# A trunk kernel on one core: P of two head groups turned by VectorE and DRAM instead of TensorE, a hand-ordered opening, and moved waits

## The chip, the cores and the metric

The kernel runs on one core of a Trainium2 chip. The core has five engines that run their own instruction queues in order: PE (TensorE, matmuls and transposes), DVE (VectorE), ACT (ScalarE), POOL (GpSimd) and SP (SyncE, which here only issues DMAs); ACT issues DMAs too. The metric is the device time of one execution in microseconds (us).

## The reference

Two layers over `x` (256 rows, width 1024), all in float32. Each layer is a half-step SwiGLU, a mixer, and another half-step SwiGLU. The mixer of layer 0 is the one that the change touches most:

```python
x = x + 0.5 * swiglu(rmsnorm(x, ffn1_norm[i]), w_gate, w_up, w_down)   # D_FF = 2816
h = rmsnorm(x, mix_norm[i])
q_s, k_s, v_s, q_m = split(h @ w_in[i])            # widths 768, 768, 768, 256
k_m, v_m = split(rmsnorm(mem, mem_norm[i]) @ w_mem_kv[i])
q_m, k_m = rmsnorm per head of 64                  # 4 memory heads, 256 keys
o_m = softmax(q_m k_m^T / 8) v_m
# layer 0: 12 heads of 64, chunks of 64 rows, each sees its own and earlier chunks
q, k = rmsnorm(q_s), rmsnorm(k_s)
s = q k^T / 8 + rel_bias[head, clip(row - key, -128, 128) + 128]
o_s = softmax(where(key chunk <= row chunk, s, -1e30)) v
# layer 1: differential attention with rotary q and k, 6 heads of 2 x 64
x = x + concat(o_s, o_m) @ w_out[i]
x = x + 0.5 * swiglu(rmsnorm(x, ffn2_norm[i]), ...)
```

## The kernel before

Every large product is made of three passes of 128x512 on PE: with a weight split into `hi` (its fp32r cast) and `lo` (the rest), and the activations likewise into `xh` and `xl`, the passes are hi·xh (L542), lo·xh (L545) and hi·xl (L548). Weights arrive by SP's DMAs in three `raw` buffers (L321), ACT casts `hi` (L367), DVE subtracts `lo` (L385). Some products of the feed-forward parts are made by Strassen sums, which the change leaves alone.

The order of the instructions on every engine is fixed when the program is built. A planner, `Flow`, runs generators ("threads"): each emits instructions, adds their cost to a planned clock (`flow.pe`, `flow.act`, `flow.dve`), and yields either a planned time at which it wants to go on or a condition (a free buffer, a free PSUM bank). Between two products of the main stream the planner lets those threads emit whose time or condition has come. So a thread's `yield flow.now + 5.0` decides only where its next instructions stand in the queues; on the chip an instruction waits for what it reads, and holds what is behind it on its engine.

**First mixer.** `qk_evac` (L1380 on) takes a projection's PSUM bank, makes squares on ACT (`sq`), sums and a power on DVE and POOL, and the normalized `qkn` on DVE (L1049); PE transposes it into `qktp` (L578), ACT and DVE copy it with its gain. q's rows are transposed by `flip`, a reversed identity, which turns their order around: so the bias of row p and key j can be read from a table by a plain stride (`load_bias`), and the P of a head group is turned back by the same `flip`. `attn_soft` makes the scores of four heads (`S`, L1487), adds the bias and takes maxima on DVE, exponentials on ACT (L1538), scales on DVE, then `p_transpose` turns P on PE into the bank `ptp` with 128x128 transposes against `flip`, ACT copies it to `PT` (L1501), and `AV` follows (L1571), with a cast on ACT and a subtract on DVE into `oT`. There are three head groups (12 heads), each for two row tiles of 128; tile 0 sees 128 keys, tile 1 sees 256. So P of a group takes 4 transposes for tile 0 and 8 for tile 1. `acc` (L542 to L548 on `oT`) is the out-projection. The memory heads' keys go through DRAM (`kd`, `kr`) and become `km` on ACT and DVE (L1192, L1195).

**DRAM trips.** `x` of the mixer's norm is already turned by DVE and DRAM in places: DVE transposes blocks of 32x32 (`xb`), a DMA of ACT's queue writes `xd`, another reads `xr`.

**Opening.** PE warms up on the identity (`warm`, L1778), transposes the first halves of x (`xtp`) and the gain row (`gps`), DVE scales (`y`, L612), ACT and DVE split, and the first products `gu` follow. `start_gain`, `start` and `loader` set planned times for these.

## Time and profile before

| | |
|---|---|
| median of three runs | 948.5 us (948.01, 948.50, 948.53) |
| profiled execution | 948.83 us |
| its span, first to last instruction | 947.0 us |
| PE busy | 940.3 us, 99% |
| DVE, ACT busy | 829.7 us, 590.8 us |
| granted TensorE clock, mean | 1.000 |
| DMA, mean over the span | 218 GB/s |

A busy PE is one with an instruction in its pipe; a product shows as 0.39 us though the next begins 0.23 us after it. So lost time on PE is read from the starts of its instructions in the timeline: a product that begins later than 0.23 us behind its forerunner has lost the difference.

### The profile page before, as it was taken

Reading aid. Unit: us, or ns where it says so; the run is one execution under the profiler, and the core shown is the slowest. Engines: PE = TensorE matmul, PEld = TensorE weight load, DVE = VectorE, ACT = ScalarE, POOL = GpSimd, SP = SyncE. Lnnn points to the kernel's source line nnn. Section 1 sums busy time; section 2 is a strip of 40 time slices with the busy share of each in tenths; the row PEclk is TensorE's granted clock in tenths of the full one; section 3 lists DMA queues with packets and bytes.
Section 4 is the critical chain, followed back from the end, with each engine's and each line's share of the span. In section 5 each row is a group of like instructions: output and inputs, shape, how many; then the busy total and the mean of one; then the engine's idle time right before and its main releaser. Section 6 shows DMA issues by size and latency. Waiting matters only on the chain. (4 is left out here: it accounts for less than half of the span.)

```text
span 947.0 us, 13323 instructions
## 1 busy us (share of the span) xinstructions
PE 940.3 (99%) x4456; PEld 773.2 (82%) x4456; DVE 829.7 (88%) x1501; ACT 590.8 (62%) x1126; POOL 108.6 (11%) x160
## 2 busy tenths in 40 slices
PE   9999999999999999999999999999999999999998
PEld 7888888887878888888888888888887788888887
DVE  6989988888777889989889899796999899998995
ACT  6656666677786746647546656563777765655671
POOL 0000038731210000000000000000334100000000
PEclk9999999999999999999999999999999999999999
DMA  9968799688525486896847679775632367589561
GB/s 296 284 212 250 228 325 329 231 268 254 178 90 164 121 258 210 266 291 225 259 143 217 214 233 290 236 252 173 203 130 76 131 219 225 188 260 329 183 217 47
DMA packets 172574, 206.13 MB, mean 218 GB/s; under 512 B 10265, under 2 KB 147290, under 8 KB 172506
## 3 DMA queue, kind: packets, MB, share of 16 engines
q1 hardware_dynamic: 169498, 202.92, 67.0%
q10 hardware_dynamic: 3008, 2.37, 0.8%
q8 instruction: 35, 0.57, 0.2%
q14 instruction: 33, 0.27, 0.1%
HBM read 190.04 MB, written 15.20 MB: 217 GB/s over the span
## 5 line engine op out<-in xcount | busy, mean ns | idle before, releaser
L367 ACT CAST hi<-raw 128x512 fp32r<-128x512 f32 (+1 forms) x466 | 334.8, 770 | 152.4 <-DMA raw<-in_ffn_w_up_dram 45.7
L385 DVE TENSOR_TENSOR lo<-raw,hi 128x512 fp32r<-128x512 f32 (+1 forms) x466 | 392.2, 877 | 23.1 <-ACT hi L367 22.5
L548 PE MATMUL gu<-hi,xl 128*128 128x512 f32 x528 | 206.0, 390 | 0.0
L542 PE MATMUL gu<-hi,xh 128*128 128x512 f32 x528 | 206.0, 390 | 0.0
L545 PE MATMUL gu<-lo,xh 128*128 128x512 f32 x528 | 205.8, 390 | 0.0
L545 PEld LDWEIGHTS gu<-lo,xh 128*128 128x128 f32 x528 | 99.2, 188 | 21.0 <-DVE lo L385 0.4
L548 PEld LDWEIGHTS gu<-hi,xl 128*128 128x128 f32 x528 | 99.3, 188 | 21.0 <-DVE xl L654 0.4
L542 PEld LDWEIGHTS gu<-hi,xh 128*128 128x128 f32 x528 | 99.4, 188 | 20.4
L548 PE MATMUL acc<-hi,ht 128*128 128x512 f32 x270 | 105.6, 391 | 0.0
L542 PE MATMUL acc<-hi,ht 128*128 128x512 f32 x270 | 105.1, 389 | 0.0
L545 PE MATMUL acc<-lo,ht 128*128 128x512 f32 x270 | 105.1, 389 | 0.0
L367 ACT CAST hi<-wsum 128x512 fp32r<-128x512 f32 x83 | 49.0, 620 | 40.0 <-DVE wsum L379 37.0
L548 PE MATMUL pj<-hi,xl 128*128 128x512 f32 x160 | 63.9, 400 | 0.0
L545 PE MATMUL pj<-lo,xh 128*128 128x512 f32 x160 | 63.6, 397 | 0.0
L542 PE MATMUL pj<-hi,xh 128*128 128x512 f32 x160 | 63.5, 397 | 0.0
L545 PEld LDWEIGHTS acc<-lo,ht 128*128 128x128 f32 x270 | 50.7, 188 | 10.6
L542 PEld LDWEIGHTS acc<-hi,ht 128*128 128x128 f32 x270 | 50.7, 188 | 10.4
L548 PEld LDWEIGHTS acc<-hi,ht 128*128 128x128 f32 x270 | 50.7, 188 | 10.4
L585 POOL TENSOR_TENSOR xr<-v,nhalf 128x1 f32<-128x1 f32 x12 | 8.6, 719 | 429.6 <-DVE v L583 429.6
L385 DVE TENSOR_TENSOR lo<-wsum,hi 128x512 fp32r<-128x512 f32 x83 | 53.7, 676 | 0.0
L728 ACT ACTIVATE sil<-gu,xr 128x256 f32<-128x256 f32 x72 | 33.8, 469 | 24.7 <-PE gu L548 23.1
L585 POOL TENSOR_TENSOR hf<-v,nhalf 128x8 f32<-128x8 f32 (+1 forms) x20 | 32.1, 1607 | 83.2 <-DVE v L583 74.1
(244 smaller groups left out, 1531.5 us busy)
## 6 DMA issues: line engine op xcount, KB each, us to landing
raw<-in_ffn_w_down_dram SPq DMA_DIRECT2D x176, 256.0 KB, 4.4
raw<-in_ffn_w_gate_dram SPq DMA_DIRECT2D x82, 512.0 KB, 4.6
raw<-in_ffn_w_up_dram SPq DMA_DIRECT2D x82, 512.0 KB, 5.2
raw<-in_w_in_dram SPq DMA_DIRECT2D x32, 512.0 KB, 5.1
hd<-hb SPq DMA_DIRECT2D x44, 256.0 KB, 4.9
hr<-hd SPq DMA_DIRECT2D x44, 256.0 KB, 5.1
raw<-in_w_out_dram SPq DMA_DIRECT2D x8, 1024.0 KB, 4.9
raw<-in_w_mem_kv_dram SPq DMA_DIRECT2D x4, 1024.0 KB, 9.0
```

The source lines that it names most:

```text
L367: nc.scalar.copy(out=it.part(0, q, w), in_=src())
L385: nc.vector.tensor_sub(it.part(1, q, w), src(), it.part(0, q, w).bitcast(F32))
L542: nc.tensor.matmul(out=ps, lhsT=xh, rhs=wh, start=start, stop=False)
L545: nc.tensor.matmul(out=ps, lhsT=xh, rhs=wl, start=False, stop=False)
L548: nc.tensor.matmul(out=ps, lhsT=xl, rhs=wh, start=False, stop=stop)
L585: nc.gpsimd.tensor_tensor(out=dst, in0=v[:, :n], in1=nhalf[:, :n], op=ALU.pow)
L728: nc.scalar.activation(sil, ps[tb][:, 0:256], AF.Silu, scale=xt.r[tb])
```

## The change

1. **No reversal.** `flip` and its use are gone. The host expands the bias to 128x12x256, so that each row has its own shifted copy, and `load_bias` reads it; the masked rows are now 0 to 63 of a tile.
2. **P of head groups 0 and 1 by a trip.** `p_transpose` stays for group 2. For groups 0 and 1 `carried` runs `trip` as a thread of its own: a 32x32 block transpose on DVE (`tb`), a DMA write to DRAM (`td`) and a DMA read back (`tr`), both issued by ACT; AV then reads `tr` in place of `PT`. `qk_evac` can use `trip` too, but has it switched off (`far = False`).
3. **Waits of threads.** The memory keys' thread goes on 9.0 us after its read of DRAM is issued, not 5.0; in the first mixer `qk_evac` waits 2.0 us more ahead of its transposes.
4. **Opening.** The five threads of the opening are written out as a list: 23 warm-up matmuls on a zeroed tile, the gain's transpose, two more, x in halves of 256 columns for row tile 0, and planned arrivals `FIRST` for the first three weight chunks. The third chunk is loaded and split in pieces of 512 columns. The planner counts PE's work double until 7.5 us (`COLD`).

```diff
     def pe(self, dur):
-        self.now += dur
+        self.now += dur * (2 if self.now < COLD else 1)
...
+    FIRST = ((4.7, 6.1, 6.9, 8.6), (10.2, 10.2, 12.1, 12.1), (15.1, 15.1, 16.6, 16.6))
...
-            pieces = (4, 2)[len(chunks)] if len(chunks) < 2 else 1
+            pieces = (4, 2, 2)[len(chunks)] if len(chunks) < 3 else 1
...
             r = from_dram(d, "kr")
-            yield flow.now + 5.0
+            yield flow.now + 9.0
...
-                nc.gpsimd.memset(b[64:128, :, 192:256], NEG)
+                nc.gpsimd.memset(b[0:64, :, 192:256], NEG)
...
+                    if typ_a:
+                        yield flow.now + 2.0
+                    yield banks.has()
+                    tp = bank("qktp")
+                    for j in range(4):
+                        t = turn(tp[:, j, :], nat[:, j * P:(j + 1) * P])
...
+        def trip(src, n):
+            yield g2.has()
+            m = n // P
+            xb = g2.take([P, 4, m, 32], F32, "tb")
+            nc.vector.transpose(out=xb.rearrange("p b m j -> p m b j"), in_=src.rearrange("p (m i b) -> p m b i", b=4, i=32))
+            t = flow.dve(n, n / 1200.0)
+            g2.give()
+            yield t + 0.1
+            d = dram.tile([4, 32, 4, m * 32], F32, tag=f"td{m}", name="td", bufs=4)
+            nc.scalar.dma_start(out=d.rearrange("a i b x -> (a i) (b x)"), in_=xb.rearrange("p b m j -> p (b m j)"))
+            flow.act(0, 0.2)
+            yield flow.now + 3.2
+            g2.give()
+            yield g2.has()
+            r = g2.take([P, 4, m * 32], F32, "tr")
+            nc.scalar.dma_start(out=r, in_=d.rearrange("a i b x -> (i b) a x"))
+            flow.act(0, 0.2)
+            yield flow.now + 3.8
+            return r.rearrange("p a (m j) -> p m a j", j=32)
...
+        def carried(src, nk, pts, e):
+            r = yield from trip(src.rearrange("p a b -> p (a b)"), 2 * nk)
+            pts[e] = r.rearrange("p (a b) c j -> p a b c j", a=2)
...
             for e in range(2):
                 yield pes[e][6]
-                pt, t = yield from p_transpose(pes[e][0], nk, bias_t is not None)
-                pts.append(pt)
+                if grp < 2 and typ_a:
+                    flow.spawn(carried(pes[e][0], nk, pts, e))
+                    continue
+                pt, t = yield from p_transpose(pes[e][0], nk)
+                pts[e] = pt
+            yield lambda: None not in pts
...
+    warm(23)
+    tp = bank("gps0")
+    nc.tensor.transpose(out=tp[:, 0, :16], in_=g1row, identity=ident[:16, :16])
+    nc.vector.tensor_copy(gcol[:, 0:16], tp[:, 0, :16])
+    warm(2)
...
+    A, B, C = (0, 1), (2, 3), range(4)
+    tpa, tpb = turned(0, A), turned(0, B)
+    first_hi(0)
+    scaled(0, tpa, A)
+    high(0, A)
+    scaled(0, tpb, B)
+    first_lo(0)
+    high(0, B)
+    low(0, A)
+    warm(4)
+    tpc = turned(1, C)
+    first_hi(1)
+    scaled(1, tpc, C)
+    low(0, B)
+    first_hi(2)
+    high(1, C)
+    first_lo(1)
+    low(1, C)
```

PE's queue at the first transposes of q and k in the first mixer, before; `pj` are the projections' banks, `qkn` the normalized q and k:

```order
L545 MATMUL pj_2350<-lo_0_2203,xh_1810 128x512
L548 MATMUL pj_2350<-hi_0_2202,xl_1812 128x512
L578 MATMUL qktp<-flip,qkn 128x128 x2
L578 MATMUL qktp<-ident,qkn 128x128 x2
L542 MATMUL pj_2350<-hi_0_2202,xh_1810 128x512
```

The same place of PE's queue now:

```order
L551 MATMUL pj_2375<-hi_0_2284,xl_1827 128x512
L545 MATMUL pj_2375<-hi_0_2284,xh_1825 128x512
L581 MATMUL qktp<-ident,qkn 128x128 x4
L548 MATMUL pj_2375<-lo_0_2285,xh_1825 128x512
L551 MATMUL pj_2375<-hi_0_2284,xl_1827 128x512
```

The four transposes stand behind 64 products of the stage where they stood behind 54.

ACT's queue while P of head group 0 is turned, before; `ptp` is the transposed P in PSUM, `PT` its copy, `oT` the AV result:

```order
L367 CAST hi_0_2500<-raw_2374 128x512 x2
L1501 COPY PT<-ptp 128x256
L1040 ACTIVATE sq<-pj_2503,xr 128x512
L1501 COPY PT<-ptp 128x256
L1501 COPY PT<-ptp 128x512 x2
L367 CAST hi_0_2620<-raw_2409 128x512
L1577 CAST oT_2625<-AV 128x2x128
```

And now, with the DMA issues of the trips; a `tr` read waits on ACT until its `td` write has landed:

```order
L368 CAST hi_0_2615<-raw_2437 128x512 x2
L1504 DMA td<-tb 128x256
L368 CAST hi_0_2649<-raw_2514 128x512
L1043 ACTIVATE sq<-pj_2499,xr 128x512
L368 CAST hi_0_2649<-raw_2514 128x512
L1510 DMA tr<-td 128x4x64
L1504 DMA td<-tb 128x512
L1510 DMA tr<-td 128x4x64
L368 CAST hi_0_2649<-raw_2514 128x512
L1504 DMA td<-tb 128x512
L368 CAST hi_0_2649<-raw_2514 128x512
L1510 DMA tr<-td 128x4x128
```

Four copies of group 0 have made room for four writes and four reads, with weight casts and a `sq` behind the reads; group 1 follows the same pattern.

PE's queue in the out-projection of the first mixer, before; `qmtp` are the memory queries' transposes, `km` the memory keys:

```order
L578 MATMUL qmtp<-ident,qmn 128x128 x2
L1571 MATMUL AV<-PT,V_2348 64x128 x2
L1571 MATMUL AV<-PT,V_2349 64x128 x2
L1571 MATMUL AV<-PT,V_2348 64x128 x2
L1571 MATMUL AV<-PT,V_2349 64x128 x2
L1487 MATMUL S<-k_2824,q_2958 128x256 x12
L542 MATMUL acc_3060<-hi_0_2757,oT_2625 128x512
```

And now:

```order
L1613 MATMUL AV<-tr,V_2373 64x128 x4
L1613 MATMUL AV<-PT,V_2373 64x128 x4
L581 MATMUL qmtp<-ident,qmn 128x128 x2
L545 MATMUL acc_3003<-hi_0_2744,oT_2749 128x512
L548 MATMUL acc_3003<-lo_0_2745,oT_2749 128x512
L1521 MATMUL S<-km_1994,qmT 128x256 x12
L551 MATMUL acc_3003<-hi_0_2744,oT_2749 128x512
L545 MATMUL acc_3000<-hi_0_2806,oT_3082 128x512
L1613 MATMUL AV<-tr,V_2373 64x128 x2
L1613 MATMUL AV<-tr,V_2374 64x128 x2
L1613 MATMUL AV<-tr,V_2373 64x128 x2
L1613 MATMUL AV<-tr,V_2374 64x128 x2
```

The memory scores `S<-km` stand two products behind the transposes of their queries; before they stood ten products behind them. AV of group 0 moved towards the out-projection: that of row tile 0 stands 71 products behind its scores, that of row tile 1 92 products. The scores of group 1 stand 10 products behind the transposes of their q and k, right behind an AV that reads `tr`; before they stood 45 products behind them.

## Rows read from the trace of the kernel before

**Rows 1.** The page's first part: busy time, share, instructions of each engine

```profile
PE 940.3 (99%) x4456; PEld 773.2 (82%) x4456; DVE 829.7 (88%) x1501; ACT 590.8 (62%) x1126; POOL 108.6 (11%) x160
```

**Rows 2.** What PE waited for: us in total, times, longest us

```profile
PE warm L1778 <- POOL ident masks.py:199: 1.4, 1, 1.4
PE qktp L578 <- DVE qkn L1049: 1.1, 1, 1.1
```

**Rows 3.** PE's timeline, opening: start us, us, engine, line, op [idle before <-releaser]

```profile
4.01 1.11 PE L578 MATMUL xtp<-ident,x 128*128 128x128 f32 x4 [0.15 <-DMA x<-in_x_dram]
5.05 0.28 PE L1762 MATMUL gps<-ident,g1row 16*128 16x16 f32 x1
...
6.71 1.06 PE L578 MATMUL xtp<-ident,x 128*128 128x128 f32 x4
7.42 0.78 PE L542 MATMUL gu<-hi,xh 128*128 128x512 f32 x1
...
8.42 0.63 PE L548 MATMUL gu<-hi,xl 128*128 128x512 f32 x1
...
11.41 0.40 PE L542 MATMUL gu<-hi,xh 128*128 128x512 f32 x1
11.64 0.39 PE L545 MATMUL gu<-lo,xh 128*128 128x512 f32 x1
```

**Rows 4.** DVE's timeline in the opening

```profile
5.58 0.69 DVE L612 TENSOR_TENSOR y<-xtp,gcol 128x512 f32<-128x512 f32 x1
...
12.03 1.46 DVE L385 TENSOR_TENSOR lo<-raw,hi 128x512 fp32r<-128x512 f32 x2 [0.44 <-ACT hi L367]
```

**Rows 5.** PE's timeline ahead of the first q and k transposes

```profile
220.63 0.39 PE L548 MATMUL pj<-hi,xl 128*128 128x512 f32 x1
222.13 0.44 PE L578 MATMUL qktp<-flip,qkn 128*128 128x128 f32 x2 [1.11 <-DVE qkn L1049]
```

**Rows 6.** DVE's timeline there

```profile
218.47 1.14 DVE L1195 SCALAR_TENSOR_TENSOR km<-kr,gcol,km 128x128 fp32r<-128x128 f32 x4 [0.97 <-ACT km L1192]
...
221.34 0.74 DVE L1049 SCALAR_TENSOR_TENSOR qkn<-pj,xr,hf 128x512 f32<-128x512 f32 x1
```

**Rows 7.** PE's timeline at one set of reversed P transposes

```profile
241.51 0.60 PE L578 MATMUL ptp<-flip,pe 128*128 128x128 f32 x4
241.87 0.48 PE L542 MATMUL pj<-hi,xh 128*128 128x512 f32 x1
242.18 0.40 PE L545 MATMUL pj<-lo,xh 128*128 128x512 f32 x1
```

**Rows 8.** Two DMA writes of turned x: count, KB, median us to landing

```profile
xd<-xb ACTq DMA_DIRECT2D x1, 256.0 KB, 5.1
...
xd<-xb ACTq DMA_DIRECT2D x1, 256.0 KB, 2.0
```

**Rows 9.** SP's timeline: one of the loads of w_out

```profile
243.12 0.37 SPq L321 DMA_DIRECT2D raw<-in_w_out_dram  x1
```

**Rows 10.** First mixer to its out-projection: PE, PEld, DVE, ACT, POOL busy; clock, DMA

```profile
208.60:278.90 70.30, 69.19 (x403) 56.07 (x401) 58.47 (x171) 50.63 (x129) 13.73 (x8) 1.00 0.57 180
```

**Rows 11.** DVE's groups: busy, mean ns of one, idle before

```profile
L623 DVE STREAM_TRANSPOSE xb<-x 128x512 f32<-128x512 f32 x4 | 4.4, 1094 | 0.0
```

**Rows 12.** PE's timeline in the second mixer's out-projection

```profile
735.58 0.40 PE L542 MATMUL acc<-hi,oT 128*128 128x512 f32 x1
736.21 1.53 PE L1487 MATMUL S<-k,q 64*128 64x256 f32 x12 [0.23 <-ACT PT L1501]
737.66 0.71 PE L1628 MATMUL AV<-V,PT 128*128 128x128 f32 x4
...
741.71 0.40 PE L545 MATMUL acc<-lo,oT 128*128 128x512 f32 x1
742.17 0.99 PE L1487 MATMUL S<-km,qmT 64*128 64x256 f32 x12
743.09 0.50 PE L548 MATMUL acc<-hi,oT 128*128 128x512 f32 x1
```

More of the change, by code (lines that the diff above doesn't have):

```diff
@@ L44 @@
 AHEAD = 0
+COLD = 7.5
 class Flow:
@@ L223 @@
     nc.gpsimd.memset(dummy, 0.0)
-    flip = const.tile([P, P], F32, name="flip")
-    nc.gpsimd.memset(flip, 0.0)
-    nc.gpsimd.affine_select(out=flip, in_=flip, compare_op=ALU.not_equal, fill=1.0, base=-(P - 1),
-                            pattern=[[1, P]], channel_multiplier=1)
     late_loads = []
@@ L575, in two_phases, with turn @@
         return t
-    def turn(dst, src, flipped=False):
-        nc.tensor.transpose(out=dst, in_=src, identity=flip if flipped else ident)
+    def turn(dst, src):
+        nc.tensor.transpose(out=dst, in_=src, identity=ident)
         return flow.pe(T_TR)
@@ L1152, in split_evac @@
         else:
-            nc.vector.scalar_tensor_tensor(out=lo, in0=src, scalar=gain, in1=hi.bitcast(F32),
-                                           op0=ALU.mult, op1=ALU.subtract)
+            far = len(src.shape) == 4
+            for o, x, y in [(lo[:, i], src[:, i], hi[:, i]) for i in range(2)] if far else [(lo, src, hi)]:
+                nc.vector.scalar_tensor_tensor(out=o, in0=x, scalar=gain, in1=y.bitcast(F32),
+                                               op0=ALU.mult, op1=ALU.subtract)
         return flow.dve(n, 0.06)
@@ L1396, in run @@
                     yield flow.dve(512)
-                yield banks.has()
-                tp = bank("qktp")
-                for j in range(4):
-                    t = turn(tp[:, j, :], nat[:, j * P:(j + 1) * P], typ_a and j < 2)
-                g2.give()
-                yield t
+                far = False
+                if far:
+                    tp = yield from trip(nat, 512)
+                    pool = g2
+                else:
+                    if typ_a:
[5 more added lines that the diff above has]
+                    g2.give()
+                    yield t
+                    pool = banks
+                a4 = lambda x: x.rearrange("p k (a j) -> p k a j", a=4) if far else x
                 gq, gk = (gcs[:, 2:3], gcol[:, GC_AK:GC_AK + 1]) if typ_a else (None, None)
@@ L1757 @@
     xt = Xt(PAIR[0, 1] is not None)
-    def start_gain():
-        yield 3.9
-        tp = bank("gps0")
-        nc.tensor.transpose(out=tp[:, 0, :16], in_=g1row, identity=ident[:16, :16])
-        yield flow.pe(T_TR)
-        nc.vector.tensor_copy(gcol[:, 0:16], tp[:, 0, :16])
-        banks.give()
-        flow.dve(16)
-        first_gain.append(True)
-        warm(2)
-        yield 5.6
-        warm(1)
-    def start(tb, hf, t):
-        yield t
-        yield from prep_half(xt, tb, hf, GC_FFN1, 3.0)
+    wz = junk[:, 0:P]
@@ L1776, in warm, with turned, scaled @@
+    nc.vector.memset(wz, 0.0)
+    wb = bank("warm")
+    banks.give()
     def warm(n):
         for _ in range(n):
-            nc.tensor.matmul(out=wb[:, 0, :], lhsT=ident, rhs=ident, start=True, stop=True)
-    wb = bank("warm")
+            nc.tensor.matmul(out=wb[:, 0, :], lhsT=wz, rhs=wz, start=True, stop=True)
+    def turned(tb, ks):
+        tp = bank("xtp")
+        for k in ks:
+            turn(tp[:, k - ks[0], :], xs[tb][:, k * P:(k + 1) * P])
+        return tp
+    def scaled(tb, tp, ks):
+        n = len(ks)
+        g = gcol[:, GC_FFN1 + ks[0]:GC_FFN1 + ks[0] + n]
+        nc.vector.tensor_tensor(out=xt.y[tb, 0][:, ks[0]:ks[0] + n], in0=tp[:, 0:n],
+                                in1=g.unsqueeze(2).broadcast_to([P, n, P]), op=ALU.mult)
+        banks.give()
+        flow.dve(n * P)
@@ L1781, with first_lo, start @@
+    def first_lo(q):
+        nc.vector.tensor_sub(items[0].part(1, q), items[0].own(q)(), items[0].part(0, q).bitcast(F32))
+        items[0].lot[q] = flow.dve(512)
+    def start(tb, t):
+        yield t
+        yield from prep_half(xt, tb, 1, GC_FFN1, 3.0)
+    warm(23)
+    tp = bank("gps0")
+    nc.tensor.transpose(out=tp[:, 0, :16], in_=g1row, identity=ident[:16, :16])
+    nc.vector.tensor_copy(gcol[:, 0:16], tp[:, 0, :16])
     banks.give()
-    warm(5)
-    flow.now = 2.7
-    flow.spawn(start_gain())
+    warm(2)
@@ L1785 @@
+    first_gain.append(True)
     for tb in range(2):
-        for hf in range(2):
-            flow.spawn(start(tb, hf, (3.4, 12.6, 5.8, 13.4)[2 * tb + hf]))
+        xt.y[tb, 0] = g2.take([P, 4, P], F32, "y")
+        flow.spawn(square(xt, tb, 0, 18.0))
+    A, B, C = (0, 1), (2, 3), range(4)
+    flow.now = 4.0
+    tpa, tpb = turned(0, A), turned(0, B)
+    flow.free.update(A=4.75, V=4.75)
+    first_hi(0)
[4 more added lines that the diff above has]
+    high(0, B)
@@ L1788 @@
+    low(0, A)
+    warm(4)
+    flow.now = 5.35
+    tpc = turned(1, C)
+    flow.free["A"] = 6.1
+    first_hi(1)
+    scaled(1, tpc, C)
+    low(0, B)
+    flow.free["A"] = 6.85
+    first_hi(2)
+    high(1, C)
+    first_lo(1)
+    low(1, C)
+    for tb, t in ((0, 13.2), (1, 14.0)):
+        flow.spawn(start(tb, t))
     flow.spawn(gain_columns())
```

53 lines of the change are left out of this document (35 added, 18 removed).

## The prediction

> **What bounds the kernel now.** I read the page's busy shares first, then what PE waited for, then PE's timeline where the change acts. PE is busy in 99% of the span [rows 1]; the one longer wait after the opening that the list of waits has is 1.1 us for `qkn` [rows 2]. So the kernel is a chain of products on PE, and an edit is worth what it takes off that chain: instructions of PE that go, waits of PE that go or come. DVE and ACT have room on the average, but in the first mixer up to its out-projection DVE is busy 58.47 and ACT 50.63 of 70.30 us [rows 10], so a queue there can be late though its engine isn't full. The measure of a loss is the pitch: a product begins 0.23 us behind its forerunner (11.41 to 11.64 in [rows 3]); what is longer is lost, also where no wait is named.
>
> The sum is made against the profiled execution, 948.83 us. It is 0.33 us above the median, 948.5, and I take 0.33 off at the end.
>
> **The change part by part.**
>
> *Opening.* Before, DVE's first scaling `y` begins at 5.58 [rows 4], because the gain's transpose stands behind four transposes of x and comes at 5.05 [rows 3]. From then on DVE has next to no idle time until 12.03, where it waits 0.44 us for ACT's `hi` of a later chunk [rows 4]; so in this stretch DVE paces what PE can start. Now the gain comes ahead of x, and `y` is in two halves, the first of which needs two of the four transposes: 4.01 plus half of 1.11 is 4.57, and with 0.1 us from PE to DVE about 4.65. DVE starts 5.58 − 4.65 = 0.93 us earlier with the same work (a half more of fixed costs here and there), and I take −0.9. The best case is PE's own: four transposes of the second row tile (0.71 us, from 6.71 to 7.42 in [rows 3]) right behind the first four (end 5.12) would let the first product start at 5.83 instead of 7.42, −1.6. The worst: the loads don't come earlier; the wait at 12.03 then grows by what was won, the gain is 0, and a product that runs at the early pitch (7.42 to 8.42 are two, 0.50 each) instead of 0.23 costs 0.27: +0.3. The warm-ups on zeros run while PE has nothing to do: the 1.4 us that `warm` waited for the identity [rows 2] lie ahead of x's arrival at 4.01 and are worth nothing.
>
> *Transposes of P.* 24 go: four and eight for each of two head groups. One set costs PE: from 241.51 to the second product behind it at 242.18 are 0.67 us, less one pitch 0.23, 0.44 for four [rows 7], or 0.11 each. 24 × 0.11 = −2.6. This is on the chain of PE, and nothing hides it: I count it in full. The 12 reversed transposes of q cost the same with either identity.
>
> *The wait ahead of q and k.* The transposes of the first `qkn` begin at 222.13, 1.50 us behind the product at 220.63 [rows 5]; less a pitch, 1.27 lost. DVE shows why: four `km` (1.14 us from 218.47) and weight splits stand ahead of `qkn`, which begins at 221.34 and ends at 222.08 [rows 6]. Now the transposes stand ten products later, 2.3 us, and `km` is behind: `qkn` has 3.4 us more than it had, so the wait goes, −1.3. What is late next: the gain copies `qk` and `k` on ACT, which feed the scores of that group, later by 2.3 us too. If the wait only moves there it is 0; the bounds are −1.3 and 0.
>
> *What comes in its place on ACT and DVE.* Eight `PT` copies go from ACT, off the chain. DVE gets eight block transposes, four of 512 columns at 1.09 us [rows 11] and four of 256, which I estimate at half to three fifths of that: some 7 us on an engine with 70.30 − 58.47 = 11.8 us idle in the stage [rows 10]. That fits, but makes DVE's queue later for the weight splits behind. ACT gets 16 DMA issues, and eight of them, the reads, wait in ACT's queue until their write has landed. Behind them stand weight casts `hi`, a `sq` and the `qk` copies; for those wait the products, the scores and the out-projection.
>
> How long is such a wait? The kernel's own writes of turned x through ACT's queue took 5.1 us to landing in one window beside weight loads and 2.0 us in another with little traffic [rows 8]. The planner lets 3.2 us pass between write and read. With 5.1 a read holds ACT for 1.9 us, with 2.0 not at all. The trips of the later tiles fall where SP loads w_out in transfers of 1 MB (one at 243.12 [rows 9]). I take one such hold to reach PE: the scores of group 1, which had 45 products between their transposes and themselves and now have ten (2.3 us), must wait for `qk` and `k` behind two reads. 2 × 1.9 = 3.8 us of hold, less the 2.3 us and part of the slack that the casts have: about +1.2, from 0 to 3.
>
> The Trainium skill, in "DMA: Bandwidth & Descriptors", section "Queues, rings and completion order", says that each DMA engine takes turns between the queues that have work for it, packet by packet; a write on ACT's queue then never stands behind SP's whole loads. By that rule the hold would be small and this term 0, and the sum 1.2 us lower. The row of 5.1 us beside the loads [rows 8] speaks against taking it so far, the 2.0 us in a quiet window doesn't decide it.
>
> *The out-projection, packed closer.* AV of the carried groups and the memory heads move into it. A place where a block of small matmuls follows its producer closely is seen in the second mixer: the block at 736.21 begins 0.63 us behind a product and takes 1.45 us to the next block, while the same count at 742.17 begins 0.46 us behind and takes 0.92 [rows 12]; so tight 0.7 us more, loose nothing. In the order I count five tight places (two products between `qmtp` and `S<-km` twice where there were ten, AV right behind a read's landing twice, the last AV). At 0.4 each, a little above the middle of 0 and 0.7 as the row of 0.7 had its wait at 0.23 only: +2.0, from 0 to 3. One more change between products and small blocks costs the 0.23 us by which 742.17 is late behind 741.71 [rows 12]: +0.2, up to 0.8.
>
> *At nothing:* the later `km` (needed only in the out-projection, tens of us later, and a cover of that size doesn't go); the host's bias table (another DMA pattern on SP of the same size, long ahead of its use); the third chunk in pieces; the masked rows.
>
> Sum: −0.9 − 2.6 − 1.3 + 0.2 + 1.2 + 2.0 = −1.4. 948.83 − 1.4 = 947.4, less 0.33: **947.1 us**. With all good ends (−1.6 − 2.6 − 1.3) it is 943.0, with all bad ones (+0.3 − 2.6 + 0 + 0.8 + 6) 953.0.
>
> **The rivals.**
>
> *B, the new waits don't come.* The reads find their data landed, and the out-projection's blocks have their inputs. For it: 2.0 us in the quiet window [rows 8], ACT idle 19.7 us of the stage [rows 10], and the planner's 3.2 us. Against: the 5.1 us. Then −0.9 − 2.6 − 1.3 + 0.2 = −4.6, 943.9 us after the 0.33; with one small wait left 944.9. I take 944.0 to 945.5.
>
> *C, slower: ACT is held at the reads.* If the writes take 5 us at five of the eight or more, ACT stands 8 to 15 us still (1.9 each, and what a read behind another read adds), of the 19.7 us that it has idle in the stage; but its casts stand behind it in order, and PE needs one about every 0.7 us (three passes). If half of 14 us reaches PE, +7: −4.6 + 7 = +2.4, about 951. It decides from the point at which a write takes over 4.5 us at most reads. Against: such a landing time is seen at one write only.
>
> *D, the early part is worth nothing.* The opening meets its loads (DMA was waited for at 12.03 through `hi`) and the wait for `qkn` moves on to the scores, so 0 and 0; with −2.6 for the transposes, +0.2 and about +2.0 for new waits it is −0.4: 948.1, to 948.6.
>
> **How the numbers follow.** The forecast (A) has 0.45, with its own range 946.0 to 948.2; B 0.30, C 0.13, D 0.12. A difference that can be told from none is 0.2%, 1.9 us, so faster is below 946.6 and slower above 950.4. B is faster whole, of A 0.12: 0.42. C is slower: 0.13. The rest, 0.33 of A and 0.12 of D, is 0.45 for the same. The range of 944.2 to 949.2 leaves out C and the lower end of B, near 2 in 10.
>
> **What would show it.** The first product near 6 to 6.5 us instead of 7.42, and the thirteenth near 10.5 instead of 11.41; no wait at `qktp`; no `ptp` for two groups; `td` landing in 2 to 3.5 us (B) or near 5 (A, C), with ACT idle ahead of `tr` issues; waits of PE at the scores of group 1 and at `S<-km` of about 1 us and half a us. The forecast is wrong if PE shows no such wait (B), or if `hi` of the first mixer's products is waited for (C), or if the first product isn't earlier by 0.5 us (D).

## The result, and the profile after

| | before | after |
|---|---|---|
| median (runs, lowest to highest) | 948.58 us (6, 948.01 to 949.37) | 953.23 us (6, 950.65 to 955.51) |
| profiled execution, span | 948.83, 947.0 us | 950.65, 948.8 us |

The ratio is 1.0043 [1.003, 1.0056]: the changed kernel is slower, and the time lies above the range of the prediction. In a later set of runs on the chip it took 950.76 us (10 runs, 949.79 to 952.36) beside 948.66 of before, 1.0024 [1.0015, 1.0033]. The profiled execution was the fastest of its six, so its trace shows 1.8 us of loss; the rest is spread, which comes up again below. The first median, 953.23, lies even above the 953.0 that the prediction gave as the sum of all its bad ends.

The page's first row of after, beside [rows 1], tells nothing of it: PE is as busy as before, 940.1 us. The granted TensorE clock has a mean of 1.000 in both profiles, so the loss isn't the clock's either.

The starts of products tell more. Both kernels have 3852 products of 128x512 in the same succession of stages, so the nth of one can be set against the nth of the other (negative: after is ahead):

| product | start before, us | start after, us | after − before |
|---|---|---|---|
| first | 7.42 | 5.99 | −1.43 |
| 60th to 240th | 23.24 to 64.04 | 22.26 to 63.06 | −0.98 |
| 300th | 77.64 | 77.52 | −0.12 |
| 360th | 91.66 | 93.15 | +1.49 |
| 480th | 118.86 | 122.14 | +3.28 |
| 540th to 840th | 132.46 to 200.46 | 135.96 to 203.96 | +3.50 |
| 1260th, behind the first mixer | 323.07 | 324.71 | +1.64 |
| 3480th | 857.44 | 859.13 | +1.69 |

So the opening gained 1.0 us, as forecast; 4.5 us were lost between 64 and 132 us, in the rest of the first feed-forward part, of which no term of the prediction speaks; the first mixer gave back 1.9; behind it nothing moves. (A number of a product here counts from 0.) Where the 4.5 us fall differs from run to run: in the profile that experiment 12 took of the same kernel PE keeps a lead of 1.1 us up to 86 us, and 3.6 us are lost from there to 126.

What PE waited for in after, beside [rows 2] (line, releaser: us in total, times, longest):

```profile
PE gu L548 <- DVE lo L388: 1.5, 3, 0.9
...
PE qktp L581 <- DVE qkn L1052: 0.7, 1, 0.7
...
PE gu L548 <- DVE lo L1839: 0.4, 1, 0.4
PE S L1521 <- ACT pe L1576: 0.3, 1, 0.3
```

`gu` waits for `lo`, the low parts of weights that DVE makes; before had no such row. The list holds 1.9 us of such waits, 0.4 of them in the opening (L1839); the pitch shows the rest, since a product that is late without idle time of PE isn't listed. PE's timeline at the longest of these waits:

```profile
90.56 0.39 PE L545 MATMUL gu<-hi,xh 128*128 128x512 f32 x1
91.87 0.50 PE L548 MATMUL gu<-lo,xh 128*128 128x512 f32 x1 [0.92 <-DVE lo L388]
```

The second begins 1.31 us behind the first, 1.08 more than the pitch. What was DVE doing? Its timeline in after ahead of this place:

```profile
79.85 3.49 DVE L388 TENSOR_TENSOR lo<-raw,hi 128x1024 fp32r<-128x1024 f32 x3
83.25 0.69 DVE L897 TENSOR_TENSOR gu_v<-gu_u,pair_m 128x512 f32<-128x512 f32 x1
...
86.29 1.22 DVE L388 TENSOR_TENSOR lo<-raw,hi 128x1024 fp32r<-128x1024 f32 x1
...
90.20 0.48 DVE L734 SCALAR_TENSOR_TENSOR h<-gu,xr,sil 128x256 f32<-128x256 f32 x1 [1.23 <-ACT sil L731]
90.60 1.22 DVE L388 TENSOR_TENSOR lo<-raw,hi 128x1024 fp32r<-128x1024 f32 x1
```

The `lo` that is late is the last row: it stands behind an `h`, and that waited 1.23 us for ACT's `sil`. ACT's timeline tells why `sil` was late:

```profile
83.96 0.47 ACT L731 ACTIVATE sil<-gu,xr 128x256 f32<-128x256 f32 x1 [0.24 <-PE gu L551]
87.79 2.00 ACT L368 CAST hi<-raw 128x1024 fp32r<-128x1024 f32 x2 [3.36 <-DMA raw<-in_ffn_w_up_dram]
89.70 0.46 ACT L731 ACTIVATE sil<-gu,xr 128x256 f32<-128x256 f32 x1
```

It stands behind two casts that waited 3.36 us for a load of weights. So weights arrive too late. The rows of DVE above show one place where that is made. A chunk's four `lo` are split up: three at 79.85, then the sums `gu_v` (the first at 83.25, three more behind it), and only then the fourth at 86.29, which ends at 87.5. The `raw` buffer is free for the next load when the fourth is made, and SP, which has that load in turn, stands still:

```profile
83.21 0.35 SPq L337 DMA_DIRECT2D grow<-in_b_subln_dram  x1
87.57 0.35 SPq L319 DMA_DIRECT2D raw<-in_ffn_w_gate_dram  x1
```

From 83.56 to 87.57 SP issues nothing: 4.0 us without a new load. Between 106 and 115 us the products that need these weights lose 1.2 us in five places, behind `lo`; experiment 18 shows that this place is the cause. In before DVE had the four together at this place of the program, ahead of the sums:

```profile
76.06 4.62 DVE L385 TENSOR_TENSOR lo<-raw,hi 128x1024 fp32r<-128x1024 f32 x4
...
83.47 0.68 DVE L894 TENSOR_TENSOR gu_v<-gu_u,pair_m 128x512 f32<-128x512 f32 x1
```

and SP's next load followed as they ended:

```profile
80.70 0.35 SPq L321 DMA_DIRECT2D raw<-in_ffn_w_gate_dram  x1
```

DVE does the same work in both. Nothing of these instructions is in the diff: the planner gave them another place because the opening's planned times are different. Three more late places of that kind stand ahead of this one. A write `hd` on SP, which waits for DVE, now stands ahead of eight loads; in before these loads were issued from 50.29 to 55.43, now from 56.55 to 60.19 (SP's timeline in after: the write, and the first of them):

```profile
56.16 0.34 SPq L748 DMA_DIRECT2D hd<-hb  x1
56.55 0.43 SPq L319 DMA_DIRECT2D raw<-in_ffn_w_gate_dram  x1
```

Two `lo` of an earlier chunk end at 39.6 and 43.9 us instead of 35.2 and 36.3, behind other work of DVE. And the four squares of the norm on ACT (`junk`) now stand in one row ahead of weight casts, so that DVE idles, first for the squares and then for a cast behind them (its timeline in after):

```profile
20.69 0.16 DVE L679 TENSOR_TENSOR sst<-xss 128x1 f32<-128x1 f32 x1 [1.12 <-ACT junk L670]
...
22.44 2.36 DVE L388 TENSOR_TENSOR lo<-raw,hi 128x1024 fp32r<-128x1024 f32 x2 [0.65 <-ACT hi L368]
```

The opening itself went as forecast. PE's timeline of after, to be held against [rows 3]:

```profile
3.58 0.26 PE L1848 MATMUL gps<-ident,g1row 16*128 16x16 f32 x1
...
5.99 0.78 PE L545 MATMUL gu<-hi,xh 128*128 128x512 f32 x1
6.57 0.63 PE L548 MATMUL gu<-lo,xh 128*128 128x512 f32 x1
6.99 0.45 PE L551 MATMUL gu<-hi,xl 128*128 128x512 f32 x1
...
8.06 0.50 PE L548 MATMUL gu<-lo,xh 128*128 128x512 f32 x1 [0.38 <-DVE lo L1839]
...
10.04 0.39 PE L545 MATMUL gu<-hi,xh 128*128 128x512 f32 x1
```

The gain's transpose at 3.58 and the first half of x free DVE's `y` at 4.63 (4.65 was forecast), the first product starts at 5.99; the thirteenth is at 10.04 instead of 11.41. The first ones still run at 0.58 and 0.42 us, and one waits 0.38 for `lo`. DVE's timeline beside [rows 4]:

```profile
4.63 0.85 DVE L1819 TENSOR_TENSOR y<-xtp,gcol 128x256 f32<-128x256 f32 x2 [0.58 <-PE xtp L581]
...
11.13 1.29 DVE L388 TENSOR_TENSOR lo<-raw,hi 128x512 fp32r<-128x512 f32 x2 [0.98 <-ACT hi L368]
```

The wait for ACT's `hi` at 12.03 is still there, earlier and longer (0.98 us).

In the mixer, PE at the second set of q and k transposes, to be held against [rows 5]:

```profile
233.03 0.39 PE L551 MATMUL pj<-hi,xl 128*128 128x512 f32 x1
234.14 0.63 PE L581 MATMUL qktp<-ident,qkn 128*128 128x128 f32 x4 [0.72 <-DVE qkn L1052]
```

The first set waits no longer; this one comes 1.11 us behind its forerunner, 0.88 over the pitch. DVE's timeline shows five weight splits ahead of `qkn`, where [rows 6] had `km`:

```profile
230.23 3.10 DVE L388 TENSOR_TENSOR lo<-raw,hi 128x512 fp32r<-128x512 f32 x5
233.25 0.74 DVE L1052 SCALAR_TENSOR_TENSOR qkn<-pj,xr,hf 128x512 f32<-128x512 f32 x1
```

A read of a trip holds ACT (ACT's timeline; `td` is the write, `tr` the read):

```profile
249.27 0.33 ACTq L1504 DMA_DIRECT2D td<-tb  x1
...
255.42 0.38 ACTq L1510 DMA_DIRECT2D tr<-td  x1
255.85 0.69 ACT L1043 ACTIVATE sq<-pj,xr 128x512 f32<-128x512 f32 x1 [3.54 <-DMA td<-tb]
```

The third `td` is issued at 249.27, its `tr` at 255.42, and ACT stood 3.54 us, with a `sq` and the gain copies of group 1 behind. But the scores that were feared for begin right behind AV, which has its `tr` (PE's timeline):

```profile
257.40 0.66 PE L1613 MATMUL AV<-tr,V 128*64 128x128 f32 x8
257.99 0.71 PE L1521 MATMUL S<-qk 64*128 64x128 f32 x8
```

The memory scores `S<-km` have one wait, the 0.3 us for ACT's `pe` in the list above; with its pitch about 0.5 us is lost there.

Beside [rows 10] and [rows 11], the stage's busy times (PE, PEld, DVE, ACT, POOL) and the block transposes of 512 columns:

```profile
208.60:278.90 70.30, 69.58 (x365) 56.16 (x364) 65.01 (x181) 52.36 (x127) 15.11 (x10) 1.00 0.70 221
```

```profile
L1499 DVE STREAM_TRANSPOSE tb<-pe 128x512 f32<-128x512 f32 x4 | 4.2, 1085 | 0.0
```

DVE has 6.5 us more work in the window, as estimated (some 7); the transposes of 256 columns take 632 ns.

### The profile page after: what moved, and what is told of

It is laid out like the page before. It is cut to its first block, busy times and chain, and to the rows that moved or that the text cites. A ratio compares the mean times of both kernels' runs of the same rounds, so it can differ in the third digit from the quotient of the medians.

```text
span 948.8 us, 13335 instructions
## 1 busy us (share of the span) xinstructions
PE 940.1 (99%) x4445; PEld 769.5 (81%) x4445; DVE 835.0 (88%) x1514; ACT 587.8 (62%) x1121; POOL 106.2 (11%) x158
## 5 line engine op out<-in xcount | busy, mean ns | idle before, releaser
L734 DVE SCALAR_TENSOR_TENSOR h<-gu,xr,sil 128x256 f32<-128x256 f32 x72 | 34.4, 478 | 10.8 <-ACT sil L731 10.8
```

The lines of the kernel that those rows point to most:

```text
L734: nc.vector.scalar_tensor_tensor(out=h, in0=ps[tb][:, 256:512], scalar=xt.r[tb], in1=sil, op0=ALU.mult, op1=ALU.mult)
```

## The experiments

All are compared with the kernel before, run beside them on the same chip. A time is a median; the ratio is the one on record with its 95% interval, and isn't the quotient of the two medians (for experiment 1 that quotient is 0.9986). The runs were made in five sets (1 to 4, 5 to 8, 9 to 12, 13 to 16, 17 and 18), in which before took 948.66 to 948.89 us; so a difference of two sets is uncertain by some 0.2 us besides its spread, and the changed kernel itself took 953.23 in one set and 950.76 in another. "Lost pitch" is what the products' and small blocks' pitch exceeds its undisturbed value by in a stretch of the profiled execution (for products 0.227 us); between 72 and 130 us it is 0.2 us in before and 4.1 in after.

**1. The mixer's part alone**: the changed kernel with the opening of before, code and planned times.

```diff
-COLD = 7.5
+COLD = 0.0
-            pieces = (4, 2, 2)[len(chunks)] if len(chunks) < 3 else 1
+            pieces = (4, 2)[len(chunks)] if len(chunks) < 2 else 1
...
+    def start_gain():
+        yield 3.9
```

> The opening of the kernel before with the mixer part of the change (no reversal, trips, later memory keys, margin). In the changed kernel's trace PE is 1.0 us ahead at 64 us, 3.5 us behind at 132 us and 1.64 us behind from the first mixer's end on, so the mixer gave 1.9 us back and all of the loss lies ahead of it. Theory (the loss comes with the opening): 948.6 - 1.9 = 946.7, runs within 0.5 us of each other. Rival (the mixer's new waits cost, as the recorded case C had it): 949 or more.

947.55 us (11 runs, 946.62 to 950.91) against 948.89: 0.9992 [0.9983, 1.0]. Lost pitch between 72 and 130 us is 0.2 again; the lead grows by 1.9 us in the mixer as it does in after. So the loss sits in the opening.

**2. The opening alone**: the changed kernel with the mixer of before. Of the lines that this brings back:

```diff
+    flip = const.tile([P, P], F32, name="flip")
...
-            yield flow.now + 9.0
+            yield flow.now + 5.0
```

> The kernel before with the new opening alone (warm-up on zeros, hand order, planned arrivals, third chunk in pieces, the doubled planned cost of early PE work). Theory (the opening carries the loss): 948.6 - 1.0 + 4.5 = 952 in the quickest run and, as in the changed kernel, runs that lie 3 to 5 us apart, since PE then waits for splits that wait for loads. Rival (the opening is worth its 1.0 us and the loss needs the mixer part too): 947.6.

955.99 us (5 runs) against 948.89: 1.007 [1.0058, 1.0082], the slowest of all. The lead of 1.3 us that it has from 22 to 63 us becomes 4.2 us of delay at 205. Another 2.8 are lost in the mixer, though its code is that of before. Most of that is at the first transposes of q and k: they begin 2.30 us behind the product ahead of them (225.87 to 228.17; 1.50 us in before), and from 228.28 to 231.69 us the granted clock is 0.50, which costs some 1.5 us more.

**3. The four squares earlier on ACT, and nothing else moved.**

```diff
+                if i == 1 and q % 2 == 0:
+                    ahead(q // 2, 0)      # the square of this row tile, ahead of the cast
```

> The changed kernel with one thing moved: ACT's four squares of x, which stand in one row ahead of the fourth chunk's casts (18.4 to 21.4 us), are issued between earlier instructions of ACT; no other instruction of any engine changes its place. Theory (these 3.0 us hold the casts, DVE stands idle 2.2 us from 19.6 to 22.4, a buffer comes free late and the loads and splits of the first feed-forward part never catch up): the splits come some 2 us earlier, PE's waits for lo between 72 and 127 us fall from 4.5 us to 2 or less, median 949 to 951. Rival 1 (the third chunk's loads in four pieces are the cause) and rival 2 (the re-planned order of splits on DVE is the cause): unchanged, 952 to 954.

952.95 us (12 runs, 948.16 to 954.71): 1.0034 [1.0021, 1.0046]. The theory of the squares falls: they alone aren't the cause.

**4. The third chunk loaded whole**, in two DMAs instead of four, nothing else moved.

```diff
+                if i == 2:
+                    if j < 2:
+                        dst, src = whole2[j]
+                        nc.sync.dma_start(out=dst(c.raw), in_=src)
```

> The changed kernel with the third chunk loaded in two transfers of 512 KB as before, not in four of 256 KB; no other instruction changes its place. Theory (squares on ACT): unchanged within the spread, 951 to 954. Rival 1 (the pieces delay SP's later loads, whose fourth chunk is issued 0.3 to 1.1 us later than before): the waits for lo go, 949 to 950. Rival 2 (re-planned order of splits): unchanged.

951.79 us (7 runs, 951.09 to 955.74): 1.0036 [1.0025, 1.0048]. Not the pieces. Its profile fell on a run of 955.04 us, and there the lost pitch between 72 and 130 us is 7.7 us: this long run lost its time in the same stretch. A part of it is the clock. PE's timeline of this kernel, and a window with its busy times, granted clock and DMA (as in [rows 10]):

```profile
72.94 0.50 PE L552 MATMUL gu<-hi,xh 128*128 128x512 f32 x1 [1.70 <-ACT hi L373]
...
74.69 0.63 PE L558 MATMUL gu<-hi,xl 128*128 128x512 f32 x1
75.12 0.63 PE L552 MATMUL gu<-hi,xh 128*128 128x512 f32 x1
```

```profile
74.33:77.74 3.41, 3.41 (x9) 2.64 (x10) 3.41 (x7) 0.86 (x2) 0.00 (x0) 0.50 0.22 45
```

Between 70.84 and 74.20 PE begins one product, the first row. Then the granted clock is 0.50, the lower of its two levels (1.2 instead of 2.4 GHz), for 3.41 us; products begin 0.43 us apart there instead of 0.23, which costs some 1.6 us.

**5 and 16. The new opening in the old order**: zero warm-ups, the gain's transpose first, row tile 0 scaled in halves, with the planner's times, and so all later places, as they were. Run twice.

```diff
+    warm(23)
+    tp0 = bank("gps0")
+    nc.tensor.transpose(out=tp0[:, 0, :16], in_=g1row, identity=ident[:16, :16])
...
+        if cut:
+            for j in range(2):
+                nc.vector.tensor_tensor(out=y[:, 2 * j:2 * j + 2], in0=tps[j][:, 0:2],
```

> The mixer part with the new opening's instructions (zeros to warm up, the gain's transpose first, x of row tile 0 in halves) put into the order of the kernel before: but for these rows of the first 7 us no instruction of any engine stands elsewhere than in the run with the mixer part alone. Theory now (the loss is the order into which the planner puts loads, casts, splits and the feed-forward part's other DVE work once the opening's planned times differ; squares and pieces are not it): PE keeps its lead, 0 waits for lo between 20 and 205 us, 0.5 to 1.0 us below the mixer part alone, 946.5 to 947. Rival (the loads set the pace of the first feed-forward part, and a PE that begins earlier only waits for lo later): the lead is gone at 130 us, 947.5. Rival (the new opening's own instructions slow the start): 951 or more.

> The new opening in the old order once more, on the same chip as the run with the write ahead: 945.5 to 947.

945.89 us (7 runs, 945.3 to 947.06), 0.997 [0.9959, 0.9981]; again 945.96 (9 runs), 0.9973 [0.9963, 0.9982]. This is the version that beats both kernels: 2.8 us below before, and 4.9 below the 950.76 of the changed kernel. It has the mixer of after; its early lead is 0.43 us (0.84 in 16), less than after's 0.98, and it keeps it to 214 us. So the same kind of opening isn't harmful, its order behind it is.

**6 and 10. All of P on PE again**, in the mixer-only kernel and in the best one.

```diff
-                if grp < 2 and typ_a:
+                if grp < 0 and typ_a:
```

> The mixer part with all P transposed on PE (no trips through DRAM), opening and order of the kernel before. Theory (the trips are worth their 24 transposes, 2.6 us, less what the new waits on ACT and in the out-projection take, 1 to 2): 948.5 to 949.5. Rival (the mixer's gain is the margin for q and k and the later memory keys alone): 947 to 947.5, as with the trips.

> The new opening's instructions in the order of before, without reversal, with margin and later keys, all P transposed on PE: the best opening with the mixer that had no trips. Theory (trips and PE transposes cost the same, as 947.2 against 947.5 had it): 945.5 to 946, as with the trips (945.9), and a smaller spread of the runs than theirs. Rival (the trips gain once PE comes earlier): 947.

947.19 us (11 runs, 946.95 to 947.51), 0.9984 [0.9975, 0.9992], against 947.55 with trips; and 946.98 (11 runs), 0.9983 [0.9974, 0.9991], against 945.89 with them. The trips are worth between −1.1 and +0.4 us by these medians, not the 2.6 of the transposes they save; in both pairs the intervals overlap. One wait of PE in the mixer-only kernel says what comes in their place (columns as above):

```profile
PE S L1516 <- ACT qk L1419: 1.0, 1, 1.0
```

It is at the scores of group 1, and ACT's timeline ahead of it shows the hold that the prediction feared:

```profile
252.03 0.38 ACTq L1505 DMA_DIRECT2D tr<-td  x1
252.46 0.69 ACT L1038 ACTIVATE sq<-pj,xr 128x512 f32<-128x512 f32 x1 [5.61 <-PE pj L546]
```

ACT was idle 5.6 us ahead of the `sq`. The profile names PE's `pj` as its releaser, but that had long been done: what stands ahead of the `sq` in ACT's queue is the `tr` at 252.03, which has to wait for its `td`, and `qk` comes behind, at 253.39 and 253.76. Without trips the wait is gone.

**7. Trips without the margin**: the mixer-only kernel with the memory keys' 5.0 us back and no 2.0 us ahead of the transposes of q and k.

```diff
-            yield flow.now + 9.0
+            yield flow.now + 5.0
...
-                    if typ_a:
-                        yield flow.now + 2.0
```

> The mixer part with the trips but without the 2.0 us margin for q and k and with the memory keys at 5.0 us again; opening and order before as in the kernel before. Theory (margin and later keys take away the wait of 1.1 to 1.3 us ahead of the first qktp): that wait is back, 948 to 949. Rival (the wait only moves): 947.5.

948.62 us (11 runs, 948.2 to 949.22): 0.9997 [0.9988, 1.0006]; 1.1 slower than with them by the medians, though the intervals overlap. Two rows of its waits:

```profile
PE gu L563 <- ACT xh L648: 1.7, 1, 1.7
...
PE qktp L576 <- DVE qkn L1047: 0.9, 1, 0.9
```

The wait for `qkn` is back, and one of 1.7 us for `xh` behind the mixer.

**8. The squares planned earlier**, everything behind re-planned.

```diff
-        flow.spawn(square(xt, tb, 0, 18.0))
+        flow.spawn(square(xt, tb, 0, (9.0, 11.5)[tb]))
```

> The changed kernel with the planned time of the first two squares of x moved from 18.0 to 9.0 and 11.5 us, so that the planner orders everything behind them anew (in the run with squares early only these four instructions moved). Theory (the order decides): another order with the same opening gives another loss, waits for lo between 72 and 130 us of anything from 0 to 7 us and a time away from 952.9 by more than 1 us. Rival (the earlier start or the pieces decide, whatever the order): 952 to 954.

947.08 us (11 runs, 945.14 to 948.85): 0.9982 [0.9973, 0.9991]. With the whole opening of after; its lead of 1.31 us holds from 22 to 200 us. Experiment 3 moved these squares forward too, kept all else, and won nothing. So it is the other order of what follows that helps here, and a lead as large as after's isn't lost by itself.

**9 and 11. Two splits ahead**: the two `lo` that ended at 39.6 and 43.9 us stand ahead of other DVE work, alone, and with the squares of 3.

```diff
+    def hurry():
+        it = items[7]
+        for src, q, w, dep in it.units:
+            if it.hi is not None and it.hit[q] is not None and it.lot[q] is None and (7, q) not in early:
+                early.add((7, q))
+                nc.vector.tensor_sub(it.part(1, q, w), src(), it.part(0, q, w).bitcast(F32))
```

> The changed kernel with two of DVE's splits lo of one weight chunk (1.2 us each) moved ahead of the four sums y on x that feed the Strassen products; no other instruction of any engine changes its place. In the changed kernel these two splits end at 39.6 and 43.9 us, since the sums and xf stand ahead of them, in the kernel before at 35.2 and 36.3; the buffer that they free lets SP load the chunk after next, at 44.0 against 36.3. Theory (this place in DVE's queue makes the loads late, and PE's waits for lo between 72 and 130 us follow from it): that load comes at about 37 to 38.5, the waits fall from 4.4 us to 1 or less, 949 to 950. Rival (the whole order is late in many places, this is one of them): 951 to 952.5. Rival (it has nothing to do with this place): 953.

> The changed kernel with both moves: the two splits ahead of the sums on DVE, and the four squares of x spread between earlier instructions on ACT. Theory (the late buffer is the cause, the squares add some 2 us of lateness to the same chain): 947.5 to 949, less than with either move alone. Rival (many late places): 951 or more.

952.37 us (5 runs), 1.004 [1.0029, 1.0052]: the load came earlier, the later places were as late as before. With the squares 950.86 (10 runs, 948.42 to 953.71), 1.0025 [1.0013, 1.0038], the same as the changed kernel. That two early places explain it falls.

**12. The changed kernel again**, as the yardstick for these.

> The changed kernel as it is, beside the two runs with moves on the same chip: 951 to 954, the yardstick for them.

950.76 us, as given above.

**13 and 14. The write `hd` behind the eight loads on SP**, alone, and with the splits and the squares.

```diff
+            if writes[0] == 4:
+                held.append(put)      # issued behind the eighth load
+            else:
+                put()
```

> The changed kernel with one DMA of SP moved: the fourth write hd of the feed-forward part's turned h, which waits for DVE (SP stands 3.7 us ahead of it, 52.4 to 56.2 us), is issued behind the eight loads of a weight chunk that stand right behind it, not ahead of them; nothing else moves on any engine. All kernels whose PE waited for lo between 72 and 130 us (changed, opening only, squares early, chunk whole, two splits ahead, both moves) have this write ahead of the eight loads; the kernel before, mixer only, the new opening in the old order and the re-planned squares have it behind. Theory: the eight loads come at about 51 to 52 us instead of 56.5, the waits for lo fall from 4.4 us to 1 or less, 948 to 949. Rival (many places): a little less, 950 to 952.

> The changed kernel with all three moves that change no plan: the hd write behind the loads, the two splits ahead of the sums, the squares spread. Theory (the write is the cause, the others don't matter): as with the write alone, 948 to 949. Rival (late places add up): clearly below the write alone, 947 or less, with the write alone above 949.

951.52 us (12 runs, 949.08 to 954.89), 1.0028 [1.0017, 1.0039]: alone it does nothing. All three: 950.51 (11 runs), 1.0016 [1.0008, 1.0025]. In the profile of the three together the lead of 1.43 us holds to 90 us instead of 64; then 2.3 us are lost between 90 and 119. But the changed kernel holds its lead to 86 us in the profile of 12 as well, so that this comes from the moves isn't shown.

**15. The other way round**: in the best kernel the write ahead of the loads.

```diff
+                if eights[0] >= 3 and writes[0] < 4:
+                    held.append(put)      # a load, until the write is issued
```

> The other way round: the new opening in the old order with that one hd write moved ahead of the eight loads and of the chunk behind them; nothing else moves. Theory: the loads wait on SP for DVE's h, PE waits for lo behind 72 us appear, 3 to 5 us: 949 to 951. Rival (the place of the write doesn't matter): 946, as without the move.

948.57 us (11 runs, 946.62 to 951.33), 0.9994 [0.9985, 1.0002]: 2.6 us slower than the same kernel without it. SP's timeline of the kernel with the write ahead, and without:

```profile
57.39 0.35 SPq L760 DMA_DIRECT2D hd<-hb  x1
57.79 0.43 SPq L321 DMA_DIRECT2D raw<-in_ffn_w_gate_dram  x1
```

```profile
51.43 0.34 SPq L319 DMA_DIRECT2D raw<-in_ffn_w_gate_dram  x1
```

The loads that followed at 51.43 come at 57.79, behind the write, which waits for DVE until 57.39. That is one late place by itself, priced by the medians, with a larger hold than the 3.7 us of after. Its profile fell on its longest run, 951.33 us, 4.8 more than that of 16; 1.5 us of them are lost between 72 and 130 us, the rest in the opening, at 207 us and between 365 and 478, and that the late loads reach so far isn't shown.

**17 and 18. One split ahead of the sums**: the fourth `lo` of the chunk that stood behind the `gu_v`, with the three moves of 14, and alone.

```diff
+            if (l, nm) == (0, 1):
+                hurry_one()      # one pending lo, ahead of the gu_v sums
```

> The changed kernel with the three moves of the run before (hd write behind the loads, two splits ahead of the sums, squares spread) and a fourth: on DVE one split lo is put ahead of the four sums gu_v (2.7 us) and an h that stand between it and its three forerunners; in the changed kernel it ends at 87.4 us, and SP loads the next weight chunk only then, 4.0 us idle; in the kernel before the four splits stand together, end at 80.6, and SP isn't idle there. Theory (several late places of the new order add up, this one takes the waits between 88 and 113 us): of the 2.7 us of waits that the three moves leave about 2 go, 950.5 becomes 948 to 949. Rival (this place doesn't matter either): 950 to 951.

> The changed kernel with this fourth move alone. Theory (late places add up, and one alone helps a part): 949 to 951, PE's waits at 110 to 114 us gone. Rival (this is the one place that matters): 948 or less. Rival (it doesn't matter): 951 to 953.

947.83 us (11 runs), 0.9987 [0.9977, 0.9997]; and alone 948.61 (11 runs, 946.75 to 951.07), 0.9996 [0.9986, 1.0005]. One DVE instruction in another place, five instructions earlier, is worth 2.1 us against the 950.76 of the changed kernel, whose interval (1.0015 to 1.0033) lies wholly above its interval. DVE's and SP's timelines of this kernel:

```profile
79.73 3.49 DVE L399 TENSOR_TENSOR lo<-raw,hi 128x1024 fp32r<-128x1024 f32 x3
83.13 1.22 DVE L379 TENSOR_TENSOR lo<-raw,hi 128x1024 fp32r<-128x1024 f32 x1
84.27 0.68 DVE L908 TENSOR_TENSOR gu_v<-gu_u,pair_m 128x512 f32<-128x512 f32 x1
```

```profile
84.38 0.35 SPq L319 DMA_DIRECT2D raw<-in_ffn_w_gate_dram  x1
```

The four `lo` stand together, SP goes on at 84.38 instead of 87.57. In its profile, nothing is lost from 107 us on, where after lost another 1.4; the loss between 63 and 93 us (from −1.27 to +1.17) stays. In all nine profiles that have after's order here without this move (after, 2, 3, 4, 9, 11 to 14) PE loses 1.6 to 3.2 us behind the 400th product, at about 102 us; in 17 and 18 it loses nothing.

What stays open is the share of each late place, since they add up and hide each other (13 is worth nothing alone, 15 costs 2.6), and which of the opening's edits (`COLD`, `FIRST`, the pieces, the list) turned the order; they weren't tried one by one. The spread of the runs is open too. In the profile of a long run (4) it is lost in the first feed-forward part, some 1.6 us of it to the clock. But the mixer-only kernel, whose profile loses nothing there, spreads by 4.3 us, and by 0.6 without trips (6); as it spreads by 1.0 with trips and without the margin (7), a share of the trips isn't shown. In the profiles of 8 and 15 some 1.5 us more are lost at about 436 us, behind an `h` of DVE; why wasn't followed up.

## Why the prediction was wrong, point by point

- **The opening, −0.9: right where it was worked out, wrong as the whole price.** Measured −0.98, with `y` at 4.63; that it came so close is partly luck, as PE leads by 0.96 to 1.36 us in other profiles with this opening (13, 9). The step that failed is what the sum left out: it let the opening's effect end with the wait at about 12 us (worst end +0.3) and had no term, not even at nothing, for the order of the instructions behind. (The pieces of the third chunk stood at nothing without a reason; 4 bears that out.) But the edits to the opening also change the planner's clock (`COLD`, `FIRST`), and with it the order of `lo`, `hi`, squares, sums and loads as far as 130 us. That cost 4.5 us in the profile; experiments 1 and 2 put the loss with the opening, 5 and 16 with the order and not with the opening's instructions, 18 shows one instruction of it.
- **The profile had the warning.** A row of the windows of before that the prediction didn't look at (PE, PEld, DVE, ACT, POOL):

```profile
72.00:92.00 20.00, 20.00 (x89) 16.29 (x88) 19.93 (x28) 12.21 (x16) 0.00 (x0) 1.00 0.76 236
```

DVE was busy 19.93 of 20 us there and PE waited for nothing: whatever comes late on DVE in such a stage has no idle time to be made up from (a reading of the row, which no run tested by itself). The argument that DVE has room "on the average" hid this; I looked for a full queue only in the mixer.
- **24 transposes, −2.6: right in kind.** The `ptp` of two groups are gone. What the exchange is worth as a whole, with its new waits, is between −1.1 and +0.4 us (6 and 10); what the transposes alone gave isn't shown.
- **The wait ahead of q and k, −1.3: too much.** The first set's 1.27 went, 0.88 came at the second, behind five splits on DVE: −0.4. Not the scores of the group were next, but the next `qkn`. Margin and later keys together are worth 1.1 by the medians (7).
- **New waits, +1.2 and +2.0, and +0.2 for one more block: too much.** The mixer as a whole gave −1.87, and if the transposes gave their 2.6, and the wait 0.4, all of these cost 1.1 instead of 3.4. Of five tight places one waited, `S<-km`, for about 0.5. I had taken the middle between a block that waits and one that doesn't, for each of five.
- **The hold of ACT: right in kind, off PE's chain in this profile.** A `td` was waited for 3.54 us, more than the 1.9 taken, and PE didn't wait for what stood behind it; in the profile of experiment 1 it did, 1.0 us. Rival C came to about 951, by holds at five or more of the eight reads: a number not far off, by a wrong cause, since with the old opening the same trips leave the kernel at 947.55 (1). The mixer's 1.9 us lie between the 0.5 of my case A and the 3.7 of B. No case had the mechanism that decided.

## What to carry to other kernels

Where a planner sets the order, an edit's price isn't only in the place that it touches: hold the new order of every engine that feeds the bound one against the old one down to the next point where all wait for each other, first in the stages where the feeder is full. In such a stage, look for the instruction that frees a buffer (here the last of four splits) and ask what now stands ahead of it. And try a change of instructions and a change of order apart: here much the same instructions gave 945.9 us in the old order and 950.8 in the new.

## What the runs showed of the hardware

- A DMA trip in the stage with the bulk loads of w_out was slow and uneven: 6.1 us from the issue of a write to that of its read (249.27 to 255.42 above). Of after's sixteen DMAs of trips the trace has the landing of four: reads 6.0, 5.4 and 3.0 us, a write 1.7 us. The prediction weighed a rule of the Trainium skill ("DMA: Bandwidth & Descriptors", section "Queues, rings and completion order"): each DMA engine takes turns between the queues that have work for it, packet by packet. No run here shows the packets of the two queues in turn, so the rule is neither borne out nor contradicted; the hold, which would be small by it, was 3.54 us.
- Twenty-three warm-up matmuls from 0.98 to 3.6 us did not bring the first products to their later pitch: they start 0.58 and 0.42 us apart at 5.99, 6.57 and 6.99, while the later pitch is 0.23. The second of them is 0.63 us long and 0.42 ahead of the next, like the products at a granted clock of 0.50 in the profile of 4 (0.63 and 0.43); so these probably ran at the lower level too, but the trace has no record of the granted clock ahead of 7.1 us.
- A wait of PE can cost more than its length. In the profiles of 4 and 2 the granted clock fell to 0.50 for 3.41 us right behind a wait (1.70 us for `hi` and, one product later, 0.76 for `lo`; 1.91 for `qkn`), at a price of some 1.5 us each. A mean over the span hardly shows it. Of the 134 runs of before beside the experiments the four with a mean granted clock of 0.997 or 0.998 are the four longest, 950.81 to 951.61 us; the others, at 0.999 or 1.000, took 948.09 to 949.52.
- The kernels with late loads were uneven: 949.08 to 954.89 us in twelve runs of one kernel (13). The clock isn't all of that: eight of the twelve runs of 3 took 952.67 to 954.71 at 0.999 or 1.000. What else it is stays open.
